# Attention in a two-layer backbone: the third key tile's shaping moved behind group 0's fifth block, query roundings and norms one block later

## The chip, the cores and the metric

The kernel runs on one core of a Trainium2 chip. The metric is the time of one execution in microseconds on the device; what is given is the median of several runs. The profile comes from one further execution, recorded by the hardware profiler.

## What is computed

Two layers of a flow-matching backbone over 512 latent tokens with 256 context tokens, width 1024. Layer 0 mixes tokens by attention, layer 1 by retention; each layer has a gated feed-forward part after it. The change concerns layer 0's attention only:

```python
q_x = rope_2d(rms_norm(q_x.reshape(B, S, N_HEADS, HEAD_DIM), q_gain), tables)
k_x = rope_2d(rms_norm(k_x.reshape(B, S, N_KV_HEADS, HEAD_DIM), k_gain), tables)
k_c = rms_norm(k_c.reshape(B, L, N_KV_HEADS, HEAD_DIM), k_gain)
...
p = jax.nn.softmax(jnp.concatenate([s_ctx, s_loc, sink_col], axis=-1), axis=-1)
return (jnp.einsum('bkgqn,bnkd->bqkgd', p[..., :L], v_c)
        + jnp.einsum('bkgqn,bnkd->bqkgd', p[..., L:L + band], vb))
```

There are 16 query heads of 64 elements and 4 key groups, so that a group g serves heads 4g to 4g+3. Latent queries, in blocks of 128, attend to a band of at most 384 latent keys and all 256 context keys; context queries (two blocks) attend to the context alone. Queries and latent keys are normed and rotated (rope); a learned sink enters each softmax.

## The kernel before

The order of instructions on each engine is decided by a scheduler that reads the program top to bottom and fills engines by its own estimates; only the first part of the kernel and one stretch on TensorE have an order written out by hand. The helper `after` (L91) adds an ordering edge, without a wait of its own, from one instruction to another.

*Pools.* `ap` is the working pool with tags such as "tt" and "pr"; `rp` with tag "res" holds residual rows in 12 buffers. A tile taken from a tag waits for an earlier tile of the same buffer to be done with. "res" buffers also take the attention output before the output projection (`o_raw`), and the reloaded residual (`cres`).

*Keys.* Three normed key tiles are kept in `kn`, each 128 x 512: `kn[0]` has the latent keys of groups 0 and 1, `kn[1]` the context keys, `kn[2]` the latent keys of groups 2 and 3. ScalarE squares each into `ksq` (L529) and scales it by the gain (L530). `rope_key` (L532) rotates a tile on VectorE: a shuffle and three two-input operations (L535 to L538). `key_factor` (L540) sums squares with a matmul (L542), gets the norm's factor in `neg_half_rstd` (L194 to L200: ScalarE's ln, exp and square, VectorE's two steps) and multiplies (L545). `key_parts` (L547) splits a group's 64 rows into a rounded part on ScalarE (L550, L551) and a remainder on VectorE (L553, L554), since matmul operands are taken in two parts. All three tiles are shaped before the loop over groups.

*Query tiles.* `make_q(j)` returns four pieces for heads 2j and 2j+1: `first`, `second` and `third` hold the projection of the latent and of the context stream (24 matmuls each, L147 to L149), and `shape` of each, which scales, squares and rotates on ScalarE, VectorE and GpSimd and then rounds: two casts on ScalarE (L598, L599) and two remainders on VectorE (L600, L601) for each stream. `norms` sums squares by 12-column matmuls (L610) and works out the factors and the sink column (L199, L200, L613, L617).

*Blocks.* `attend(g, s, b)` does one block of 128 queries of group g: four heads' scores (`score`: matmuls S at L703, the masked reduction with running lower bound on VectorE at L704, the exponential on ScalarE at L101, the scaling on GpSimd at L717), the transposes (`turn`: L726, copied out by ScalarE and VectorE in turn at L728), and the value products (`output`: pO at L740). Blocks go in the order `latent + context` (L0 to L3, C0, C1) in groups 0 and 1, then L0, L1, C0, L2, L3, C1 in group 2 and C0, L0, C1, L1, L2, L3 in group 3. Behind blocks 1 and 3 of groups 0 to 2 the loop calls `make_q` for the next group's two tiles. `make_q(0)` and `make_q(1)` stand ahead of the loop.

Of the kernel before, what the change touches and what calls it, by code (L numbers as in the profile page):

```python
# [44 lines left out]
PRB = 9  # L45
TTB = 8
# [3 lines left out]
def dit_kernel(ctx, tc, xT, cT, crow, small, consts, masks, tabs0, tabs1, jtab, adaQ, adaN, adaT, wst, out):  # L50
    nc = tc.nc
# [10 lines left out]
    def T(pool, cols, tag, bufs, dt=F32):  # L62
        return pool.tile([P, cols], dt, tag=tag, bufs=bufs, name=tag)
# [309 lines left out]
    raw = []  # L373
# [148 lines left out]


    kx, kc = {}, {}
    kn = [T(ap, 512, "tt", TTB) for _ in range(3)]
    ksq = [T(ap, 656, "pr", PRB)[:, :512] for _ in range(3)]
    off_grid(ap, 16)
    for a, b, o in zip(kn, ksq, (kvx[0], kvc, kvx[1])):
        nc.scalar.activation(b, o, AF.Square)  # L529
        nc.scalar.activation(a, o, AF.Identity, scale=qk_gain[:, 1:2])  # L530

    def rope_key(t):  # L532

        yy = T(ap, 512, "tt", TTB)
        nc.vector.stream_shuffle(yy, t, swap16)  # L535
        nc.vector.tensor_tensor(t, t, rope0[:, 0:512], op=mult)
        nc.vector.tensor_tensor(yy, yy, rope0[:, 512:1024], op=mult)
        nc.vector.tensor_tensor(t, t, yy, op=add)  # L538

    def key_factor(i):  # L540
        tot = pT()
        nc.tensor.matmul(tot, bd, ksq[i], start=True, stop=True)  # L542
        y = T(ap, 656, "pr", PRB)[:, :512]
        neg_half_rstd(y, ksq[i], tot, HD)
        nc.vector.tensor_tensor(kn[i], kn[i], y, op=mult)  # L545

    def key_parts(e, src, tag="k", bufs=8):  # L547
        k1, k2 = T(akv, 512, tag, bufs, F32R), T(akv, 512, tag, bufs, F32R)
        src = src[64 * e:64 * e + 64, :]
        nc.scalar.copy(k1[0:64, :], src)  # L550
        nc.scalar.copy(k2[64:128, :], src)  # L551
        hi_same = (k1[0:64, :], k2[64:128, :])[e]
        nc.vector.tensor_tensor(k1[64:128, :], src, hi_same, op=sub)  # L553
        nc.vector.tensor_tensor(k2[0:64, :], src, hi_same, op=sub)  # L554
        return k1, k2

    q, stats = {}, {}

    def make_q(j, raw=None):

        if raw is None:
            w = next_w(ap, 0)
            parts_of = lambda k: (w[0][:, k * P:(k + 1) * P], w[1][:, k * P:(k + 1) * P])
        else:

            rows = [[T(ap, 656, "pr", PRB, F32R)[:, :512] for _ in range(2)] for _ in range(2)]
            for i, (hi, lo) in enumerate(rows):
                split(raw[:, i * 512:(i + 1) * 512], hi, lo)  # L570
            parts_of = lambda k: [t[:, k % 4 * P:(k % 4 + 1) * P] for t in rows[k // 4]]
        qs = T(ap, 64, "qs", 4)[:, 0:36].rearrange("p (f n) -> p f n", f=3)
        sqs, o = [], [None, None]

        def part(s, k0, k1):
            if k0 == 0:
                o[s] = pj(NTOK[s])
            for k in range(k0, k1):
                mm3(o[s], parts_of(k), h[s][k], k == 0, k == KT - 1)

        def shape(s):
            n = NTOK[s]
            sq, qn = t_sq(n), t_hn(n)
            nc.scalar.activation(qn, o[s], AF.Identity, scale=qk_gain[:, 0:1])
            nc.scalar.activation(sq, o[s], AF.Square)
            sqs.append(sq)
            if s == 0:
                sw = t_y(s)
                nc.vector.stream_shuffle(sw, qn, swap16)
                nc.gpsimd.tensor_tensor(qn, qn, rope0[:, 0:512], op=mult)  # L590
                nc.vector.tensor_tensor(sw, sw, rope0[:, 512:1024], op=mult)
                nc.vector.tensor_tensor(qn, qn, sw, op=add)
            qa = T(ap, 512, "q", 9, F32R)
            if s == 0:
                qb = T(ap, 512, "q", 9, F32R)
            else:
                qa, qb = qa[:, 0:SC], qa[:, SC:2 * SC]
            nc.scalar.copy(qa[0:64, :], qn[0:64, :])  # L598
            nc.scalar.copy(qb[64:128, :], qn[64:128, :])  # L599
            nc.vector.tensor_tensor(qa[64:128, :], qn[0:64, :], qa[0:64, :], op=sub)  # L600
            nc.vector.tensor_tensor(qb[0:64, :], qn[64:128, :], qb[64:128, :], op=sub)  # L601
            q[2 * j, s] = qa
            q[2 * j + 1, s] = qb

        def norms():
            tot = pj(12)
            for s, sq in enumerate(sqs):
                for b in range(NTOK[s] // P):
                    c = 8 * s + 2 * b
                    nc.tensor.matmul(tot[:, c:c + 2], sq[:, b * P:(b + 1) * P], bd[:, 0:P:64], start=True, stop=True)  # L610
            y, u, z = qs[:, 0], qs[:, 1], qs[:, 2]
            neg_half_rstd(y, z, tot, HD)
            nc.vector.scalar_tensor_tensor(u, tot, HD * EPS, y, add, mult)  # L613
            ue = u.rearrange("p (b e) -> p e b", e=2)
            for e in range(2):
                hd = 2 * j + e
                nc.vector.tensor_scalar(ue[:, e], ue[:, e], nsink[:, hd:hd + 1], -4.0 / HD, op0=mult, op1=mult)  # L617
                stats[hd] = qs

        def first():  # L620
            part(0, 0, 5)

        def second():
            part(0, 5, KT)
            shape(0)
            part(1, 0, 3)

        def third():
            part(1, 3, KT)
            shape(1)  # L630

        return [first, second, third, norms]
# [124 lines left out]
    def attend(g, s, b):  # L757
        blk = Block(g, s, b)
        for i in range(4):
            blk.score(i)  # L760
        for ki in range(len(blk.keys)):
            blk.turn(ki)
        blk.output()
        return blk.copy
# [13 lines left out]

    for piece in make_q(1):
        piece()  # L780
    rope_key(kn[2])
    key_factor(2)
    for e in range(2):
        kx[2 + e] = key_parts(e, kn[2])


    dec = sm_t[:, C_DEC:C_DEC + 8]
    lg = cp.tile([P, 8], F32, name="lg")
# [26 lines left out]
    def context_out(d, w):  # L815
# [9 lines left out]
    parts_o = [p for sb in ((0, 0, 0), (0, 1, 0), (1, 1, 0), (2, 1, 0), (0, 0, 1), (1, 0, 0), (1, 0, 1),  # L825
                            (2, 0, 0), (2, 0, 1)) for p in splits_o(*sb)]
    PARTS_AT = {(2, 4): 2, (2, 5): 3, (3, 0): 3, (3, 1): 2, (3, 2): 2, (3, 3): 2, (3, 4): 2, (3, 5): 2}
    for g in range(NKV):
        final = g == NKV - 1
        for i, (s, b) in enumerate((latent + context, latent + context, mixed, late)[g]):  # L830
            copy = attend(g, s, b)
            if not final and i in (1, 3):
                for piece in make_q(2 * g + 2 + i // 3):
                    piece()
            if (g, i) >= SPLIT_AT:
                first = len(parts_o) == 18
                for _ in range(PARTS_AT[g, i]):
                    parts_o.pop(0)([copy])
                if first:
                    wo0 = wpos[0]  # L840
                    cres = load_stream(1)
            for d in {3: early[:1], 4: early[1:3], 5: early[3:]}.get(i, ()) if final else ():
                wpos[0] = wo0 + d
                wo_w[d] = next_w(ap, 0)
                context_out(d, wo_w[d])
# [12 lines left out]
    for d4 in range(0, KT, 4):  # L858
# [4 lines left out]
        for d in range(d4, d4 + 4):  # L863
            o = pj(SX)
# [1054 lines left out]
```

## Time and profile before

| what | value |
|---|---|
| runs | 1747.34, 1749.5, 1747.12 us; median 1747.34 us |
| profiled execution: span from first to last instruction | 1744.4 us |
| mean granted clock of TensorE | 0.999 |
| instructions | 27605 |
| data moved | 203.54 MB, mean 117 GB/s |
| stretch of the attention blocks | about 97 to 318 us of the span |

The span is the profiled execution's own time from first to last instruction; the runs' time contains what lies around it as well. In rows of the profile, PE is TensorE's matmuls, PEld its weight loads, DVE is VectorE, ACT is ScalarE, POOL is GpSimd, SP is SyncE. "L12" is line 12 of the kernel; a helper's line stands for all who call it, so a tile's name tells them apart. A bracket or an arrow "<-" behind a time names what ended the idle time ahead of the instruction.

### The profile page before, as it was taken

What the parts mean: (1) busy time and instruction counts of PE and PEld (TensorE: products, weight loads), DVE (VectorE), ACT (ScalarE), POOL (GpSimd) and SP (SyncE); (2) the same over time, 40 slices, a digit from 0 to 9 for tenths busy, and PEclk for the clock granted to TensorE, in tenths of its full rate; (3) what the DMA queues carried; (4) which work ended last, traced back from release to release, by engine and by line L of the source; (5) the groups of instructions that cost most, each with busy time, mean ns of one, the idle gap of its engine ahead of it and who ended that gap; (6) DMA issues with size and microseconds to landing.
All of it is one profiled execution on the core that took longest, in us unless ns stands there. A gap on an engine that the chain in (4) does not pass through costs nothing.

```text
span 1744.4 us, 27605 instructions
## 1 busy us (share of the span) xinstructions
PE 1712.7 (98%) x10876; PEld 1527.8 (88%) x10876; DVE 1350.5 (77%) x2368; ACT 846.3 (49%) x1492; POOL 131.0 (8%) x270
## 2 busy tenths in 40 slices
PE   7999999999999999999999999999999999999999
PEld 5777777899999999999988888898898899999997
DVE  6697778788778788787889858758768798777774
ACT  5576667465433334342456534525525565445442
POOL 0035435000000000000000000000000000000000
PEclk9999999999999999999999999999999999999999
DMA  9501012533243534343423524423423224233322
GB/s 353 230 13 38 13 43 68 204 122 135 71 147 121 158 109 145 123 153 101 156 99 86 182 84 130 162 86 121 157 85 118 76 84 132 77 117 101 104 79 85
DMA packets 59602, 203.54 MB, mean 117 GB/s; under 512 B 6608, under 2 KB 6992, under 8 KB 59216
## 3 DMA queue, kind: packets, MB, share of 16 engines
q1 hardware_dynamic: 51984, 175.03, 30.9%
q0 software_dynamic: 7200, 26.22, 5.2%
q8 instruction: 85, 1.39, 0.3%
q10 hardware_dynamic: 288, 0.52, 0.1%
q14 instruction: 45, 0.37, 0.1%
HBM read 199.65 MB, written 2.10 MB: 116 GB/s over the span
## 4 chain that ended last, share of the span: by engine, by line
PE 80%; DVE 8%; DMA 5%; ACT 3%; issue 2%; POOL 1%; SPq 0%; ACTq 0%; POOLq 0%; DVEq 0%
PE Y L886 15%; PE Z L886 7%; PE pj L147 6%; PE pj L148 6%; PE pj L149 6%; PE Z L1268 6%; PE X L886 4%; PE Y L1257 3%; PE pj L1268 2%; PE pT L726 2%; PE X L1257 2%; DMA wraw<-in_wst_dram 2%; PE pO L740 2%; PE S L703 2%; DMA adan<-in_adaQ_dram 1%
## 5 line engine op out<-in xcount | busy, mean ns | idle before, releaser
L164 ACT CAST whi<-wraw 128x1024 fp32r<-128x1024 f32 x258 | 270.2, 1051 | 370.7 <-PE Z L149 88.5
L165 DVE TENSOR_TENSOR wlo<-wraw,whi 128x1024 fp32r<-128x1024 f32 x258 | 315.0, 1223 | 60.9 <-ACT whi L164 59.7
L886 PE MATMUL Y<-aq,whi 128*128 128x384 f32 x640 | 173.7, 335 | 0.5 <-ACT sq L1044 0.5
L256 DVE SCALAR_TENSOR_TENSOR res<-pj,mod,res 128x512 f32<-128x512 f32 (+1 forms) x112 | 81.5, 729 | 65.6 <-PE pj L149 65.0
L886 PEld LDWEIGHTS Y<-aq,whi 128*128 128x128 f32 x640 | 116.6, 188 | 1.7 <-ACT sq L1044 0.9
L273 DVE CUSTOM_DVE_ANT_0 y<-adaw,crow,small_sb 128x1024 bf16<-128x1024 f32 x64 | 81.9, 1280 | 36.0 <-DMA adaw<-in_adaT_dram 35.7
L886 PE MATMUL Y<-aq,wlo 128*128 128x384 f32 x320 | 107.0, 334 | 0.0
L101 ACT ACTIVATE pr<-pr,stat,qs 128x513 f32<-128x513 f32 (+2 forms) x96 | 74.4, 777 | 23.5 <-DVE stat L710 22.9
L1268 PE MATMUL Z<-whi,sA 128*128 128x512 f32 x256 | 81.0, 391 | 1.2 <-ACT gate L1454 1.2
L717 POOL TENSOR_SCALAR pr<-pr,stat 128x512 f32<-128x512 f32 (+2 forms) x96 | 70.2, 744 | 79.5 <-DVE stat L714 54.8
L147 PE MATMUL pj<-ax,whi 128*128 128x512 f32 x176 | 68.8, 391 | 0.1
L149 PE MATMUL pj<-ax,whi 128*128 128x512 f32 x176 | 68.7, 390 | 0.0
L148 PE MATMUL pj<-ax,wlo 128*128 128x512 f32 x176 | 68.5, 389 | 0.0
L147 PE MATMUL pj<-act,whi 128*128 128x512 f32 x168 | 66.0, 393 | 0.0
L148 PE MATMUL pj<-act,wlo 128*128 128x512 f32 x168 | 65.9, 392 | 0.0
L149 PE MATMUL pj<-act,whi 128*128 128x512 f32 x168 | 65.5, 390 | 0.0
L270 POOL DMA_DIRECT2D adaw<-in_adaT_dram x48 | 25.6, 533 | 514.9 <-DVE mod L273 413.6
L726 PE MATMUL pT<-const_sb,pr 128*128 128x128 f32 x352 | 57.4, 285 | 6.1 <-POOL pr L717 3.6
L886 PE MATMUL Y<-sA,whi 128*128 128x256 f32 x304 | 60.6, 282 | 0.2 <-ACT res L1721 0.2
L886 PEld LDWEIGHTS Y<-aq,wlo 128*128 128x128 f32 x320 | 60.1, 188 | 0.0
L726 PEld LDWEIGHTS pT<-const_sb,pr 128*128 128x128 f32 x352 | 39.1, 142 | 23.0 <-POOL pr L717 12.4
L1268 PEld LDWEIGHTS Z<-whi,sA 128*128 128x128 f32 x256 | 48.0, 188 | 11.7 <-ACT gate L1454 1.9
(576 smaller groups left out, 5150.3 us busy)
## 6 DMA issues: line engine op xcount, KB each, us to landing
wraw<-in_wst_dram SPq DMA_DIRECT2D x224, 512.0 KB, 3.7
adaw<-in_adaT_dram POOLq DMA_DIRECT2D x48, 512.0 KB, 3.9
wx<-in_wst_dram SPq DMA_DIRECT2D x30, 512.0 KB, 4.3
adan<-in_adaQ_dram SPq DMA_DIRECT2D x16, 512.0 KB, 8.5
adan<-in_adaN_dram SPq DMA_DIRECT2D x12, 512.0 KB, 7.8
adaw<-in_adaT_dram SPq DMA_DIRECT2D x8, 512.0 KB, 3.9
res<-in_xT_dram SPq DMA_DIRECT2D x14, 256.0 KB, 3.8
aq<-in_adaN_dram SPq DMA_DIRECT2D x12, 256.0 KB, 5.8
```

The lines of the kernel that those rows point to most:

```text
L101: ins = nc.scalar.activation(*args, **kw)
L147: nc.tensor.matmul(o, whi, xhi, start=first, stop=False)
L148: nc.tensor.matmul(o, wlo, xhi, start=False, stop=False)
L149: return nc.tensor.matmul(o, whi, xlo, start=False, stop=last)
L164: after(nc.scalar.copy(hi, t), behind)
L165: return nc.vector.tensor_tensor(lo, t, hi, op=sub)
L256: return nc.vector.scalar_tensor_tensor(res[d], o, mods[l, s][:, part, d:d + 1], res[d], mult, add)
L273: res.append(nc.vector.tensor_tensor_reduce(junk, w, cr[:, s * 1024:(s + 1) * 1024], 1.0, sm_t[:, C_ADAB + l * 48 + j:C_ADAB + l * 48 + j ...
L726: nc.tensor.transpose(tp[:, a * P:(a + 1) * P], self.pr[(0, 2, 1, 3)[a]][:, ki * P:(ki + 1) * P], ident)
L886: nc.tensor.matmul(o, p, r, start=first and k + i == 0, stop=k == 3 and i == 2, skip_group_check=not first)
L1257: ins = nc.tensor.matmul(o[:, e * SC:(e + 1) * SC], p[:, ws], r, start=first and k + e + i == 0, stop=k == 3 and i == 2, skip_group_check= ...
L1268: ins = nc.tensor.matmul(os[t], p, r, start=first and k + i == 0, stop=k == 3 and i == 2, skip_group_check=by_k or not first)
```

## The change

It changes four things in the attention stage. `kn[2]` and `ksq[2]` are taken from "res" in the pool `rp` in place of "tt" and "pr" in `ap`, as are the two scratch tiles of their shaping. The third key tile's rotation, factor and parts stand in the loop behind block 4 (C0) of group 0, its shuffle ordered behind that block's copy. Query tiles made in the loop leave their roundings out of `shape`; the roundings run at the start of `norms`. And that piece runs behind the next block, its first cast of each stream ordered behind that block's copy. Tiles 0 and 1 are made as before. The number of operations on data is the same.

```diff
-    kn = [T(ap, 512, "tt", TTB) for _ in range(3)]
-    ksq = [T(ap, 656, "pr", PRB)[:, :512] for _ in range(3)]
+    kn = [T(ap, 512, "tt", TTB) for _ in range(2)] + [T(rp, 512, "res", 12)]
+    ksq = [T(ap, 656, "pr", PRB)[:, :512] for _ in range(2)] + [T(rp, 512, "res", 12)]
...
-    def rope_key(t):
+    def rope_key(t, room=(ap, 512, "tt", TTB), behind=()):
-        yy = T(ap, 512, "tt", TTB)
-        nc.vector.stream_shuffle(yy, t, swap16)
+        yy = T(*room)
+        after(nc.vector.stream_shuffle(yy, t, swap16), behind)
...
-    def key_factor(i):
+    def key_factor(i, room=(ap, 656, "pr", PRB)):
-        y = T(ap, 656, "pr", PRB)[:, :512]
+        y = T(*room)[:, :512]
...
-    def make_q(j, raw=None):
+    def make_q(j, raw=None, apart=False):
...
+            if apart:
+                rows_of.append(qn)
+            else:
+                two_parts(s, qn)
+
+        def two_parts(s, qn, behind=()):
...
-            nc.scalar.copy(qa[0:64, :], qn[0:64, :])
+            after(nc.scalar.copy(qa[0:64, :], qn[0:64, :]), behind)
...
-        def norms():
+        def norms(behind=()):
+            for s, qn in enumerate(rows_of):
+                two_parts(s, qn, behind)
...
-    rope_key(kn[2])
-    key_factor(2)
-    for e in range(2):
-        kx[2 + e] = key_parts(e, kn[2])
...
+    later = None
     for g in range(NKV):
...
             copy = attend(g, s, b)
+            if later:
+                later([copy])
+                later = None
             if not final and i in (1, 3):
-                for piece in make_q(2 * g + 2 + i // 3):
+                *pieces, later = make_q(2 * g + 2 + i // 3, apart=True)
+                for piece in pieces:
                     piece()
+            if (g, i) == (0, 4):
+                rope_key(kn[2], (rp, 512, "res", 12), [copy])
+                key_factor(2, (rp, 512, "res", 12))
+                for e in range(2):
+                    kx[2 + e] = key_parts(e, kn[2])
```

More of the change, by code (lines that the diff above doesn't have):

```diff
@@ L572, in make_q @@
         qs = T(ap, 64, "qs", 4)[:, 0:36].rearrange("p (f n) -> p f n", f=3)
-        sqs, o = [], [None, None]
+        sqs, o, rows_of = [], [None, None], []
         def part(s, k0, k1):
```

## The prediction

> **What bounds the kernel now.** I read the busy shares and the chain that ended last first, then the attention stage in stretches, then its slices of 10 us, then what TensorE waited for.
>
> ```profile
> span 1744.4 us, 27605 instructions
> PE 1712.7 (98%) x10876; PEld 1527.8 (88%) x10876; DVE 1350.5 (77%) x2368; ACT 846.3 (49%) x1492; POOL 131.0 (8%) x270
> PE 80%; DVE 8%; DMA 5%; ACT 3%; issue 2%; POOL 1%; SPq 0%; ACTq 0%; POOLq 0%; DVEq 0%
> ```
>
> TensorE is 98% busy and holds 80% of the chain. Over the whole span it can gain little; what there is to gain are its gaps. The next rows are stretches of attention: start and end, length, then busy time of PE, PEld, DVE, ACT and POOL, and the granted clock (PEclk) behind them.
>
> ```profile
> core 0: us, PE busy (x) PEld busy (x) DVE busy (x) ACT busy (x) POOL busy (x), PEclk, DMA share, GB/s
> 97.20:148.00 50.80, 46.82 (x318) 36.82 (x316) 41.01 (x111) 34.70 (x73) 22.03 (x44) 1.00 0.07 22
> 148.00:166.00 18.00, 17.91 (x130) 14.78 (x127) 15.47 (x63) 13.45 (x37) 7.61 (x20) 1.00 0.01 1
> 166.00:206.00 40.00, 39.80 (x290) 32.37 (x289) 29.51 (x86) 27.95 (x61) 16.03 (x30) 1.00 0.08 28
> 206.00:254.00 48.00, 46.90 (x324) 37.12 (x324) 35.19 (x118) 30.60 (x74) 22.41 (x46) 1.00 0.12 39
> 254.00:273.00 19.00, 16.59 (x114) 12.45 (x112) 16.79 (x58) 14.71 (x39) 7.02 (x22) 0.91 0.20 56
> 273.00:318.00 45.00, 43.34 (x333) 35.13 (x333) 35.94 (x118) 32.57 (x83) 18.87 (x37) 1.00 0.19 60
> ...
> sum 220.80, PE 211.37 PEld 168.67 DVE 173.90 ACT 153.97 POOL 93.96; mean PE 35.23 PEld 28.11 DVE 28.98 ACT 25.66 POOL 15.66
> ```
>
> In 220.80 us TensorE is idle 9.43 us: 3.98 in the first stretch (group 0), 0.29 in the next two, 1.10, then 2.41 in the short stretch from 254 to 273 (end of group 2), 1.66 at the end. No change that only moves work can take more than these 9.4 us and what the low clock between 254 and 273 costs. The slices show which engine holds TensorE up, and that nothing behind attention gives time back:
>
> ```profile
> 120.00:130.00 10.00, 8.40 (x60) 5.36 (x56) 9.85 (x30) 7.10 (x16) 3.89 (x8) 1.00 0.00 0
> 150.00:160.00 10.00, 9.91 (x73) 8.73 (x73) 9.35 (x42) 8.51 (x26) 3.37 (x10) 1.00 0.00 0
> 160.00:170.00 10.00, 10.00 (x72) 7.16 (x70) 8.80 (x30) 6.46 (x15) 5.72 (x15) 1.00 0.01 2
> 260.00:270.00 10.00, 8.64 (x53) 6.61 (x51) 8.41 (x35) 8.09 (x23) 5.01 (x12) 0.83 0.19 54
> 320.00:330.00 10.00, 10.00 (x46) 8.28 (x45) 6.77 (x10) 6.22 (x7) 0.00 (x0) 1.00 0.90 355
> ```
>
> From 120 to 130 VectorE is 9.85 of 10 busy and TensorE 8.40: in group 0 VectorE is the bound. From 150 to 170 both are nearly full, which is where the change puts the key work. From 320 TensorE is 10.00 of 10, so an earlier end of attention goes through to the end of the kernel. Last, TensorE's waits between 97 and 148 (total, times, longest), and from the timeline the largest later one (start, length, the wait in brackets):
>
> ```profile
> PE pT L726 <- POOL pr L717: 1.7, 3, 0.7
> PE pj L610 <- ACT sq L585: 1.2, 2, 0.7
> PE pT L726 <- ACT tt L728: 0.8, 2, 0.6
> PE pO L740 <- ACT tt L728: 0.2, 1, 0.2
> ...
> 259.65 0.47 PE L703 MATMUL S<-kc,q 128*128 128x256 f32 x2 [1.05 <-DVE qs L200]
> ```
>
> The first four sum to 3.9 us, all the idle time of that stretch.
>
> **The change part by part.** Nothing is added or removed: the same shuffles, products, copies and matmuls run in another order, and two tiles live in another pool.
>
> *Third key tile, away from group 0.* Its work is listed by these rows (for one line: minimum, median and maximum ns, and the first and last start; for a group: busy us, then mean ns):
>
> ```profile
> L535 DVE STREAM_SHUFFLE tt<-tt 128x512 f32<-128x512 f32 x1 | 0.7, 722 | 0.0
> L536 DVE TENSOR_TENSOR tt<-tt,rope x2: 693/693/693, 71.1 to 76.2; 128x512 f32<-128x512 f32 x2
> L200 DVE SCALAR_TENSOR_TENSOR pr<-pr x3: 672/685/693, 78.0 to 104.3; 128x512 f32<-128x512 f32 x3
> L545 DVE TENSOR_TENSOR tt<-tt,pr x3: 685/693/693, 79.2 to 105.0; 128x512 f32<-128x512 f32 x3
> L553 DVE TENSOR_TENSOR k<-tt,k x4: 685/690/1677, 81.8 to 109.3; 64x512 fp32r<-64x512 f32 x4
> L550 ACT CAST k<-tt x4: 604/612/618, 80.2 to 107.2; 64x512 fp32r<-64x512 f32 x4
> ```
>
> On VectorE: one shuffle 0.72, three products of the rotation at 0.69, three steps of the factor (L199, L200, L545) at 0.69, four remainders (L553, L554) at 0.69: 0.72 + 10 x 0.69 = 7.6 us. ScalarE has four casts at 0.61 and three steps of the factor, put at 0.65 as my estimate from the casts and the 0.63 of L529 below: 4.4 us; TensorE has one matmul of the factor. Only the shuffle and rotation, 2.8 us, run early (76 to 79 us); factor and remainders, the other 4.8 us, run at 103 to 110, where VectorE is the bound.
>
> *Query tile 2, one block later.* Per query tile:
>
> ```profile
> L600 DVE TENSOR_TENSOR q<-hn,q 64x512 fp32r<-64x512 f32 x8 | 5.7, 717 | 2.3 <-ACT q L598 2.1
> L601 DVE TENSOR_TENSOR q<-hn,q 64x256 fp32r<-64x256 f32 x8 | 3.4, 421 | 0.2
> L598 ACT CAST q<-hn 64x512 fp32r<-64x512 f32 x8 | 4.9, 618 | 8.3 <-DVE hn L592 8.2
> L598 ACT CAST q<-hn 64x256 fp32r<-64x256 f32 x8 | 3.2, 400 | 0.1
> ```
>
> Remainders on VectorE 2 x 0.72 + 2 x 0.42 = 2.3 us, casts on ScalarE 2 x 0.62 + 2 x 0.40 = 2.0 us. Moving them from behind blocks 1 and 3 to behind the next block takes tile 2's 2.3 us out of the stretch where VectorE holds TensorE. Together VectorE has 4.8 + 2.3 = 7.1 us less to do before group 0's fifth block; in the compiled order two weight splits (L165, 1.2 us each as the row of one at 263.93 below) move up into that room, so 4.7 us net. TensorE can get back only its 3.98 us of waits; I take 3.4, since the first norms' wait (half of the 1.2 on sq) belongs to query tile 1, which is shaped as before. Bounds: 0 (another engine paces as before) and 3.98.
>
> *The two tiles moved to the other pool.* ScalarE's ops on the third key (square and gain) needed buffers that the first two keys' ops held in turn:
>
> ```profile
> 67.87 0.27 ACT L318 COPY sq<-pT 128x128 f32<-128x128 f32 x1 [6.09 <-PE pT L315]
> ...
> 70.14 0.63 ACT L529 ACTIVATE pr<-pj 128x512 f32<-128x512 f32 x1
> 70.61 0.73 ACT L530 ACTIVATE tt<-pj,qk_gain 128x512 f32<-128x512 f32 x1
> 71.18 0.66 ACT L164 CAST pr<-wraw 128x512 fp32r<-128x512 f32 x1
> 71.90 0.50 PE L147 MATMUL pj<-h,pr 128*128 128x512 f32 x1
> ```
>
> In the changed order both stand ahead of L318, in ScalarE's 6.09 us of idleness. The weight cast that releases L147 then starts up to 71.18 - 70.14 = 1.04 us sooner. I take 0.9; bounds 0 (weights or h late instead) and 1.04.
>
> *Where the key work lands.* It is queued behind the copy of group 0's fifth block, at 150 to 170, with query tile 3's remainders (2.3). VectorE there is busy 15.47 of 18 from 148 to 166 and 29.51 of 40 after it; 7.6 + 2.3 us more, against 2.53 + 10.49 us of room, fit if TensorE takes other work meanwhile. It can: the projections of query tile 4, 24 matmuls each for two streams, don't need these keys. Behind the waiting shuffle on VectorE are scores of the block C1 and then of group 1; only group 2 reads the new keys. I charge 0.8 us for the stretch, and 0.5 for group 1, where the projections are then used up sooner. Bounds 0 and 5 (rival 2). The scheduler also puts one weight DMA ahead of four loads of the residual on SP's queue; these are read only near 300, so nothing is charged.
>
> *Query tile 7, end of group 2.* These are VectorE rows between 254 and 264:
>
> ```profile
> 255.93 0.68 DVE L600 TENSOR_TENSOR q<-hn,q 64x512 fp32r<-64x512 f32 x1
> ...
> 258.75 0.74 DVE L704 CUSTOM_DVE_ANT_0 pr<-S,mask,qs 128x512 f32<-128x512 f32 x1
> ...
> 263.93 1.21 DVE L165 TENSOR_TENSOR wlo<-wraw,whi 128x1024 fp32r<-128x1024 f32 x1
> ```
>
> The remainders stand between the scores of block L3 (the fourth latent block), and S waits the 1.05 us quoted. In the changed order the remainders come after the copies of L3, and the weight split of 263.93 ahead of L3. So L3 is scored 2.3 us sooner and that wait goes; next late are group 3's first block, whose heads 14 and 15 need the remainders. I take a gain of 1.0, bounds 1.0 lost to 2.4 (all the idle time there) won.
>
> The clock is the other term there: 0.83 of full speed in the slice 260 to 270, so at most 10 x 0.17 = 1.7 us lost; I take it unchanged, since S, transposes and values stay as thin there as they are. [...]
>
> Sum: -3.4 - 0.9 + 0.8 + 0.5 - 1.0 = -4.0 us. The profiled span, 1744.4, is 2.9 us below the median 1747.34 (runs 1747.12 to 1749.5); I take the same distance for the changed kernel: span 1740.4, time 1743.3.
>
> **The rivals.** 0.2% is 3.5 us, about what a measurement here can tell from no change.
>
> 1. *The lead is handed back in groups 0 and 1.* VectorE does the 7.1 us saved early where it is 9.35 and 8.80 of 10 busy; TensorE spends its projections as filler there and has none later. For: those slices. Against: behind them VectorE has room, 29.51 busy of 40 from 166 on. Price: the 3.4 us of group 0 come back as new waits, leaving -0.9 - 1.0 = -1.9 us, 1745.4.
>
> 2. *Slower: the deferred roundings become what the next scores wait for.* The tiles shaped behind the fourth block (3, 5, 7) are rounded one block before the group that reads them; no projections stand between to cover it. The chain is casts 2.0, then remainders 2.3, 4.3 us at each of three group changes, and in group 0 7.6 us of key work queue with it. It decides if TensorE reaches the next group's third head before VectorE reaches the last remainder. If half of each chain shows (3 x 2.15 = 6.5) beside the key work's excess over the 2.5 us of room to 166 (5.1), against the gains 3.4 and 0.9, it is about +7; with only the roundings half exposed, +2.2. I put it at +5, 1752.3. For: 2.41 us of idle time stand already where group 2 ends. Against: VectorE's total there falls, and scores run one block ahead.
>
> 3. *Nothing to be measured:* what is saved before 148 is only the queue ahead of another wait (the 1.7 us on POOL's pr L717 end a chain through ScalarE and POOL that keeps its length); then the sum is -0.9 or less, 1746.4 to 1747.3.
>
> 4. *The clock.* If the drop goes, another 1.7 us are won, 1741.6; if a second appears in the new thin places, 1.7 are lost, 1745.0. It adds to any case.
>
> **How the numbers follow.** The forecast (1743.3, with its clock variants) 0.43; rival 1 0.20; rival 3 0.10; rival 2 0.27. Faster by over 0.2% takes the forecast: its lower half lies well past the bound, its upper part slips under it, which rival 1's lower part makes up: 0.43. Within 0.2%: rivals 1 and 3, 0.30. Slower: 0.27. Low end: all terms at their good bounds, -3.98 - 1.04 - 2.4 - 1.7 = -9.1, 1738.2. High end: just above rival 2's middle, 1752.5; the half of it above, 0.13, and a few hundredths below the low end are left out. Both signs carry chance, so the forecast's own range is 1740.5 to 1745.
>
> **What would show it.** Right: in the changed profile the waits on POOL pr L717 and ACT tt L728 before 140 are nearly gone, TensorE's idle time to the end of group 0's fourth block is under 1 us; L147's first matmul comes near 71.0; the keys' L553 end at 160 to 170 with TensorE over 9.5 of 10; the wait S L703 near 259 is gone. Rival 1: the same, with new idle time of 2 to 4 us between 150 and 200. Rival 2: waits of S L703 on q at the first blocks of groups 1, 2 and 3, over 2 us each. Wrong altogether: VectorE less busy from 100 to 130, but TensorE with the same gaps.

## The result: 0.15% slower, and the profile after

The changed kernel takes 1749.07 us (median of 21 runs, 1746.24 to 1754.27) against 1747.16 us before (21 runs, 1744.81 to 1749.5). The ratio is 1.0015, 95% interval 1.0009 to 1.0021: slower, clear of the measurement's own spread, by 2.6 us if the ratio is taken times 1747 (the medians lie 1.9 us apart). It stays within the 0.2% that I had called "no change", but the forecast was 4 us the other way. The profiled execution has a span of 1747.3 us.

The page of the changed kernel gives the whole:

```profile
span 1747.3 us, 27610 instructions
PE 1717.0 (98%) x10876; PEld 1530.0 (88%) x10876; DVE 1350.2 (77%) x2368; ACT 847.1 (48%) x1492; POOL 132.0 (8%) x270
...
PE 80%; DVE 9%; DMA 5%; ACT 3%; issue 2%; POOL 1%; SPq 0%; ACTq 0%; DVEq 0%; POOLq 0%
```

The counts of matmuls and of VectorE's and ScalarE's instructions are those of before. PE's busy time is 4.3 us longer for the same 10876 matmuls: part of them ran at a lower clock (0.997 of full speed in the mean of the profile, 0.999 before). The same stretches as in the prediction:

```profile
core 0: us, PE busy (x) PEld busy (x) DVE busy (x) ACT busy (x) POOL busy (x), PEclk, DMA share, GB/s
97.20:148.00 50.80, 49.62 (x349) 40.51 (x349) 36.75 (x113) 33.15 (x72) 18.75 (x42) 1.00 0.07 22
148.00:166.00 18.00, 17.41 (x113) 13.52 (x112) 16.56 (x50) 14.55 (x37) 9.45 (x18) 1.00 0.10 30
166.00:206.00 40.00, 38.72 (x280) 30.65 (x279) 34.30 (x107) 27.96 (x64) 17.54 (x35) 1.00 0.09 27
206.00:254.00 48.00, 46.76 (x322) 36.68 (x322) 36.80 (x119) 32.41 (x74) 21.14 (x47) 1.00 0.04 12
254.00:273.00 19.00, 17.01 (x108) 12.41 (x105) 14.50 (x51) 13.03 (x35) 6.43 (x16) 0.82 0.29 88
273.00:318.00 45.00, 41.01 (x314) 33.60 (x313) 35.37 (x116) 32.62 (x83) 21.04 (x39) 1.00 0.19 63
```

Group 0 is what was forecast: TensorE idle for 1.18 us to 148 where it was 3.98, with VectorE's 41.01 us down to 36.75. Then the gain is spent: 0.59 idle from 148 to 166 (0.09 before), 1.28 to 206 (0.20), about the same to 254, a clock of 0.82 in place of 0.91 to 273, and 3.99 idle in the last stretch where it was 1.66.

To see where a lead comes and goes when projections move between blocks, I follow one number: the start of each block's value products (pO) against before, less the difference in matmul time that TensorE had issued ahead of that point. The matmul time is counted by the spacing of unbroken runs in the trace: 229 ns for 512 columns, 176 for 384, 118 for 256, 80 for 128, 112 for the norms' two. It is counted from ScalarE's copy L318 on, which stands at 67.87 us before and at 68.42 in the changed kernel. Up to that copy TensorE starts the same 710 matmuls in the same order in every kernel of this document, and yet the copy stands anywhere from 66.93 to 69.33 us in the seventeen profiles: what is won or lost ahead of it differs between profiles of kernels that are alike up to there, and is not put down to the change. The lead is worked out from the two traces; minus is ahead.

```
block        g0.L1  g0.L3  g1.L1  g2.L0  g2.L2  g3.C0  g3.L3
before at    127.9  146.4  179.0  222.2  255.3  276.5  316.5
after at     123.4  140.4  184.3  223.8  252.9  277.9  319.0
lead (us)     -4.6   -4.9   -3.1   -2.1   -1.5   -0.1   +1.9
```

The lead of 4.9 us was there at 140 us. It lost 1.8 where the key work lands and group 1 starts, 1.0 in group 1, 0.6 in most of group 2, 1.5 at its end, and 2.0 in group 3, which the prediction had not touched at all. In the waits of TensorE, this is the first stretch (97 to 148) and the last (275 to 325) of the changed kernel:

```profile
PE S L711 <- DVE q L606: 0.9, 1, 0.9
PE pT L734 <- POOL pr L725: 0.2, 1, 0.2
...
PE pT L734 <- POOL pr L725: 3.4, 4, 1.4
PE pO L748 <- DVE stat L718: 0.4, 1, 0.4
```

and the last one of the kernel before:

```profile
PE pT L726 <- POOL pr L717: 1.4, 4, 0.5
```

The waits for POOL's scaling (L717, now L725) are nearly gone from group 0 (0.2 us of 1.7 is left), and in group 3 they are 2.0 us larger than before. How they come about is read on VectorE. Before, a softmax's reciprocal (L714) stands ahead of the split of an output (L165, h<-pO), which must wait for value products; GpSimd's two scalings are in between:

```profile
301.67 0.16 DVE L714 RECIPROCAL stat<-stat 128x2 f32<-128x2 f32 x1
...
301.92 1.76 POOL L717 TENSOR_SCALAR pr<-pr,stat 128x640 f32<-128x640 f32 x2 [1.12 <-DVE stat L714]
...
302.41 0.28 DVE L165 TENSOR_TENSOR h<-pO,h 128x128 fp32r<-128x128 f32 x1
```

In the changed kernel it stands behind it; VectorE, GpSimd and then TensorE, each from its own timeline:

```profile
304.38 0.29 DVE L165 TENSOR_TENSOR h<-pO,h 128x128 fp32r<-128x128 f32 x1 [1.09 <-ACT h L164]
304.59 0.15 DVE L722 RECIPROCAL stat<-stat 128x2 f32<-128x2 f32 x1
...
304.92 2.63 POOL L725 TENSOR_SCALAR pr<-pr,stat 128x640 f32<-128x640 f32 x2 [2.38 <-DVE stat L722]
...
307.60 0.44 PE L734 MATMUL pT<-const_sb,pr 128*128 128x128 f32 x2 [1.01 <-POOL pr L725]
```

VectorE is idle 1.09 us ahead of the split, a reciprocal of 0.15 us stands behind that, GpSimd is idle 2.38 us until it comes, and TensorE waits 1.01. The order is not the whole of it: the same two scalings take 2.63 us here and took 1.76 before, and nothing here shows why. The change edits no line of this stretch, so the other order is the scheduler's.

### The profile page after: what moved, and what is told of

Read it like the earlier page. It is cut to its first block, busy times and chain, and to the rows that moved or that the text cites. A ratio compares the mean times of both kernels' runs of the same rounds, so it can differ in the third digit from the quotient of the medians.

```text
span 1747.3 us, 27610 instructions
## 1 busy us (share of the span) xinstructions
PE 1717.0 (98%) x10876; PEld 1530.0 (88%) x10876; DVE 1350.2 (77%) x2368; ACT 847.1 (48%) x1492; POOL 132.0 (8%) x270
## 4 chain that ended last, share of the span: by engine, by line
PE 80%; DVE 9%; DMA 5%; ACT 3%; issue 2%; POOL 1%; SPq 0%; ACTq 0%; DVEq 0%; POOLq 0%
PE Y L899 14%; PE Z L899 7%; PE pj L147 6%; PE pj L149 6%; PE pj L148 6%; PE Z L1281 6%; PE X L899 3%; PE Y L1270 3%; DMA wraw<-in_wst_dram 2%; PE pj L1281 2%; PE pT L734 2%; PE X L1270 2%; PE pO L748 2%; PE X L147 2%; PE X L149 1%
## 5 line engine op out<-in xcount | busy, mean ns | idle before, releaser
L165 DVE TENSOR_TENSOR wlo<-wraw,whi 128x1024 fp32r<-128x1024 f32 x258 | 314.8, 1223 | 59.5 <-ACT whi L164 58.5
L725 POOL TENSOR_SCALAR pr<-pr,stat 128x512 f32<-128x512 f32 (+2 forms) x96 | 67.6, 717 | 78.4 <-DVE stat L722 66.8
L147 PE MATMUL pj<-ax,whi 128*128 128x512 f32 x176 | 68.7, 391 | 0.0
L147 PE MATMUL pj<-act,whi 128*128 128x512 f32 x168 | 66.0, 393 | 0.0
L899 PE MATMUL Y<-hx,whi 128*128 128x256 f32 x304 | 57.9, 280 | 0.1
```

The costliest lines, as they stand in the source:

```text
L147: nc.tensor.matmul(o, whi, xhi, start=first, stop=False)
L165: return nc.vector.tensor_tensor(lo, t, hi, op=sub)
L899: nc.tensor.matmul(o, p, r, start=first and k + i == 0, stop=k == 3 and i == 2, skip_group_check=not first)
```

## The experiments

Two kinds of number are given: the ratio to the kernel before in runs on the same chip, with its 95% interval, and the lead at some blocks, by the count above, from one profile each. Kernels whose programs are the same up to a block agree in their leads there to about 0.2 us, with one exception: the profile of group 1 deferred with the keys moved has a low clock at 99 to 106 us that no other has (at 103 to 104 us its 512-column matmuls start 0.43 us apart, from 106 us on 0.23), and its leads are not used. At the end of attention ten of the other fifteen leads agree with the ratios to 0.8 us, and all to 2.1. Where the expectations below speak of a lead, it is counted without L318: their 5.9 at group 0's fourth block is 5.3 here, their 3.9 at L2 is 3.4. The ratios come from four chips, so two of them are told apart only where their intervals are.

**The parts, one by one.** The edits are put against the changed kernel.

The keys' move alone:

```diff
-                *pieces, later = make_q(2 * g + 2 + i // 3, apart=True)
-                for piece in pieces:
+                for piece in make_q(2 * g + 2 + i // 3):
```

> Only the third key tile's move (its tiles in the other pool, its shaping behind group 0's fifth block); all query tiles rounded and normed at once, as before the change. Theory A (the deferred roundings are to blame: they stand behind the copy that the next scores need): the lead of group 0 stays but for the roundings' share, 3 us at the fifth block, and little is handed back later: 2 to 4 us faster than before. Theory B (the keys land where VectorE is full): a lead of some 3 us at group 0's fourth block, lost by group 1's first block: 0 to 2 us slower than before. Theory C (the losses behind group 1 come from where the scheduler happens to put weight splits and output splits, and from the clock, not from either part): lead as in A at group 1, and a change of up to 2 us either way in groups 2 and 3 that neither part explains.

Measured: 1.0014 (1.0005 to 1.0022), slower. The lead at g0.L3 is 5.3 us, more than the whole change has. It is 3.7 at g1.L0, 2.2 at g1.L1, and at g1.L2 it is gone, 1.6 behind; from there about 2.5 behind to the end of attention. That is neither A nor C, and B holds late: the loss stands mainly at two waits of 1.3 and 1.8 us, 176 and 194 us, and in a clock of 0.83 from 190 to 200 (at most 1.7). The larger wait, GpSimd and TensorE in their timelines:

```profile
191.05 1.79 POOL L590 TENSOR_TENSOR hn<-hn,rope 128x512 f32<-128x512 f32 x1 [2.06 <-DVE stat L722]
192.82 3.45 POOL L725 TENSOR_SCALAR pr<-pr,stat 128x640 f32<-128x640 f32 x4
...
194.20 0.66 PE L734 MATMUL pT<-const_sb,pr 128*128 128x128 f32 x4 [1.83 <-POOL pr L725]
```

GpSimd's part of a query tile's rotation, 1.79 us, stands ahead of the scalings that TensorE's transposes need, and by then the projections are out: ahead of g1.L1 this kernel has issued 6.3 us more matmul time than before.

The deferral alone, keys and pool as before:

```diff
-    kn = [T(ap, 512, "tt", TTB) for _ in range(2)] + [T(rp, 512, "res", 12)]
-    ksq = [T(ap, 656, "pr", PRB)[:, :512] for _ in range(2)] + [T(rp, 512, "res", 12)]
+    kn = [T(ap, 512, "tt", TTB) for _ in range(3)]
+    ksq = [T(ap, 656, "pr", PRB)[:, :512] for _ in range(3)]
...
+    rope_key(kn[2])
+    key_factor(2)
+    for e in range(2):
+        kx[2 + e] = key_parts(e, kn[2])
...
-            if (g, i) == (0, 4):
-                ...
```

> Only the query tiles' roundings and norms one block later; the third key tile in its old pool and shaped ahead of the loop. Theory A: slower than before by 2 to 5 us, waits of S on the remainders at the first blocks of groups 1, 2 and 3. Theory B: faster by 1 to 2 us, the lead of tile 2's 2.3 us of VectorE kept. Theory C: within 2 us of before, with group 3 in a different order again.

Measured: 1.0032 (1.0019 to 1.0044), by its sign as theory A has it. But the place is not A's: no wait of S on remainders stands at the groups' first blocks, and the first loss is in group 0 itself, where the deferral was to help. A lead of 2.3 at g0.L1 is 0.5 behind at g0.L3. VectorE and TensorE there:

```profile
129.97 1.20 DVE L165 TENSOR_TENSOR wlo<-wraw,whi 128x1024 fp32r<-128x1024 f32 x1
131.09 0.41 DVE L763 COPY res<-pO 128x256 f32<-128x256 f32 x1
131.42 0.15 DVE L722 RECIPROCAL stat<-stat 128x2 f32<-128x2 f32 x1
...
133.62 0.44 PE L734 MATMUL pT<-const_sb,pr 128*128 128x128 f32 x2 [1.08 <-POOL pr L725]
```

A weight split of 1.20 us, for a projection further on, stands ahead of a reciprocal that TensorE needs by way of GpSimd. The place that the remainders left was filled with longer work, less urgent than what came behind it.

The pool alone (shaping ahead of the loop, nothing deferred):

```diff
     for piece in make_q(1):
         piece()
+    rope_key(kn[2])
+    key_factor(2)
+    for e in range(2):
+        kx[2 + e] = key_parts(e, kn[2])
...
-                *pieces, later = make_q(2 * g + 2 + i // 3, apart=True)
-                for piece in pieces:
+                for piece in make_q(2 * g + 2 + i // 3):
...
-            if (g, i) == (0, 4):
-                ...
```

> Only the pool of the third key tile and its square is changed; its shaping stays ahead of the loop and its scratch tiles stay in the old pool; no query tile is deferred. By the prediction's step: L147's first matmul 0.9 us earlier (71.0 in place of 71.9) and the whole 0 to 0.9 us faster. If the lead is lost before group 0's first block: no change in the milestones from 119 us on.

Measured: 0.9988 (0.9979 to 0.9997), 2.1 us faster: the only part of the change that is a gain by itself. ScalarE and TensorE in the changed kernel, to set against the rows of the prediction (with the pool alone L147 stands at 71.38, 3.36 behind L318 at 68.02):

```profile
68.42 0.27 ACT L318 COPY sq<-pT 128x128 f32<-128x128 f32 x1 [2.32 <-PE pT L315]
...
70.69 0.65 ACT L164 CAST pr<-wraw 128x512 fp32r<-128x512 f32 x1
...
71.77 0.80 PE L147 MATMUL pj<-h,pr 128*128 128x512 f32 x1
```

From L318 to the cast it is 2.27 us, before 71.18 - 67.87 = 3.31: the 1.04 us are there, but L147 stands 3.35 behind L318 in place of 4.03, so the step gives 0.7 and not 0.9. The lead is 1.9 to 2.1 us from g0.L1 to g2.L2, more than the step, and 0.2 in the profile at attention's end; the runs have it faster all the same.

The last of the four, pool and deferral with the keys ahead of the loop:

```diff
     for piece in make_q(1):
         piece()
+    rope_key(kn[2])
+    key_factor(2)
+    for e in range(2):
+        kx[2 + e] = key_parts(e, kn[2])
...
-            if (g, i) == (0, 4):
-                ...
```

> Third key tile in the other pool, shaped ahead of the loop, and all query tiles of the loop deferred: the changed kernel without the key move. With the pool alone (0.9988), the pool and the keys (1.0014) and the whole change (1.0015) it completes the four. If what each part costs adds up: about +0.01% over the pool alone, 0.999. If the deferral costs by itself and only the key move's loss in group 1 hides it: 3 to 6 us slower than the pool alone, 1.001 to 1.003.

Measured: 1.0023 (1.0013 to 1.0033). Against the pool alone, the keys' move costs 0.26%, the deferral 0.35%, both together 0.27%. The parts do not add up; each is a cost on top of the pool, and once one of them is paid the other adds nothing that these intervals can tell.

**Where the keys land.** Keys moved, nothing deferred, and

```diff
-            if (g, i) == (0, 4):
+            if (g, i) == (1, 1):
```

with (1, 2) and (1, 4) in two more kernels.

> The third key tile's move alone (no query tile deferred), but behind the second block of group 1 (L1) in place of the fifth of group 0. If the 7.6 us of VectorE work landing at 155 to 168 cost the 6 us that the move alone lost in group 1, the loss at the two waits near 175 and 194 goes away or moves: 2 to 4 us faster than the move alone. If the loss comes of the projections being used up ahead of time as filler in group 0, the waits near 175 and 194 stay and it is as slow as the move alone.

> The same with the key work behind group 1's third block (L2), where VectorE was 4.98 of 10 busy from 190 to 200 in the kernel before. Landing theory: the lead of 5.9 us at group 0's fourth block lasts into group 2, some 4 us faster than before (1741 to 1743). Filler theory: lost in group 1 as before, no faster than 1745.

> The same with the key work behind group 1's fifth block (C0), one block ahead of the group that reads it, 200 to 215, where VectorE was 9.20 and 8.34 of 10 busy. Landing theory: the lead lasts to group 1's end and is lost at group 2's first blocks, within 2 us of before. Filler theory: lost in group 1 already.

Measured: behind (1, 1) 0.9988 (0.9979 to 0.9996), behind (1, 2) 0.9990 (0.9982 to 0.9999), behind (1, 4) 1.0006 (0.9997 to 1.0015), where (0, 4) gave 1.0014. Leads:

```
keys behind   g0.L3  g1.L1  g1.L2  g1.C1  g2.L0  g2.L2  g3.C0  g3.L3
(0, 4)         -5.3   -2.2   +1.6   +2.5   +2.7   +2.5   +2.5   +2.5
(1, 1)         -5.3   -4.7   -1.4   -1.0   -1.6   -1.8   -0.1   -0.1
(1, 2)         -5.3   -4.7   -3.4   -2.8   -3.4   -3.4   -0.9   -0.9
(1, 4)         -5.3   -4.7   -3.8   -1.7   +2.7   +4.1   +1.5   +0.8
```

Most of the lead goes where the key work lands, whichever block that is, or soon behind it: 6.8 us from g0.L3 to g1.L2 for (0, 4), 3.3 from g1.L1 to g1.L2 for (1, 1), 1.3 there for (1, 2), 4.4 from g1.C1 to g2.L0 for (1, 4). The three dear places each show a clock of 0.83 in one slice behind the landing, and (1, 2) does not. First (1, 1) and then (1, 2), from 190 to 200, and (1, 4) from 215 to 225:

```profile
190.00:200.00 10.00, 7.89 (x51) 5.89 (x52) 9.33 (x21) 8.07 (x20) 7.41 (x11) 0.83 0.18 53
```
```profile
190.00:200.00 10.00, 10.00 (x78) 8.06 (x79) 8.61 (x16) 8.13 (x17) 3.99 (x7) 1.00 0.01 2
```
```profile
215.00:225.00 10.00, 7.93 (x53) 7.35 (x50) 9.68 (x17) 5.83 (x13) 1.61 (x1) 0.83 0.01 2
```

For (1, 2) the key work begins at 194.8, and with TensorE 10.00 of 10 busy its first part is hidden; where VectorE was 9.33 or 9.68 busy, TensorE ran thin. So the landing theory holds in the main; for (1, 1) the key work was done by 186 us, and that the low clock 10 us later comes of it is argued, not shown. The filler theory is part of it: only (0, 4) had 7.5 us more matmul time out ahead of g1.L0, the others 1.1, so it was the landing there that drew the projections out. Still (1, 2) is not worth the 4 us expected: 2.5 of its 3.4 go at the end of group 2.

The same place with the deferrals kept:

> The whole change with its deferrals, but the key work behind group 1's third block. If the stretch 150 to 170 was where the change lost its lead, this keeps 1.7 us more than the changed kernel at group 1's first block and ends 1 to 2 us faster than it, 1746 to 1748 where before is 1747. If the deferral's losses in group 2 and 3 stay, it is slower than the same place without deferral (0.9990) by 2 to 4 us.

Measured: 1.0027 (1.0016 to 1.0037), so 0.37% slower than without them. The better place for the keys doesn't save the change.

**Which deferral costs.** The deferral was kept in some groups only:

```diff
-                *pieces, later = make_q(2 * g + 2 + i // 3, apart=True)
+                if g < 2:
+                    *pieces, later = make_q(2 * g + 2 + i // 3, apart=True)
+                else:
+                    pieces = make_q(2 * g + 2 + i // 3)
                 for piece in pieces:
```

with `g < 2` (groups 0 and 1, keys as in the change), `g == 1` (keys as in the change), and on the kernel with the pool alone `g == 0` and `g == 2`.

> The whole change, except that group 2 rounds and norms its two query tiles (6 and 7) at once, as before the change. Theory A: the 2 us lost between group 2's fourth block and group 3's first block come back, 2 us faster than the changed kernel. Theory B: same as the changed kernel, the loss is at group 0's end. Theory C: groups 0 and 1 as in the changed kernel; behind them the order differs again, so a time between 1745 and 1750 that goes with the waits of group 3 and with the granted clock.

> The whole change with the deferral kept for group 1 alone (tiles 4 and 5); groups 0 and 2 round at once. The two waits that cost the move alone 6 us in group 1 stand beside the shaping of tiles 4 and 5. If the deferral helps there, as the whole change's milestones suggest (it lost 1.7 us over the same blocks), this keeps the 5.9 us of lead and is 2 to 5 us faster than before. If a deferral costs wherever it stands, it is slower than the move alone, 1749 to 1751.

> The pool's change, keys ahead of the loop, and the deferral in group 0 alone (tiles 2 and 3). My prediction gave this deferral 2.3 us of VectorE's time in group 0 and so part of the 3.4 us gained. If that holds: 1 us or more ahead of the pool alone at group 0's fourth block. If the room is filled by the weight splits, as the whole deferral's trace shows at 130: no lead over the pool alone, up to 1 us behind it, and the order of group 3 as before.

> The pool's change, keys ahead of the loop, and the deferral in group 2 alone (tiles 6 and 7). All three kernels with the deferral in every group lost 2.0 us between group 3's first and last block and none without it in group 2 lost any. If that loss belongs to group 2's deferral: 2 us lost in group 3 here too, and the whole 2 to 4 us slower than the pool alone (1.000 to 1.001 of before). If it belongs to the deferrals together: group 3 as before, about 0.999.

Measured: groups 0 and 1 with the keys 1.0004 (0.9996 to 1.0013); group 1 with the keys 1.0019 (1.0010 to 1.0028); group 0 on the pool 1.0010 (1.0001 to 1.0018); group 2 on the pool 1.0010 (1.0001 to 1.0020). On the pool, each of the two deferrals is a cost against the kernel without it (0.9988). With the keys at (0, 4) nothing can be told apart: group 1 deferred (1.0019) and groups 0 and 1 deferred (1.0004) lie on either side of none deferred (1.0014), and both intervals overlap with its own.

Two of these answer questions. Group 0's deferral gives no lead at all: 2.0 us at g0.L3, as with the pool alone, and nothing is left of it at g1.L1. And group 2's deferral makes the loss in group 3. With it alone the lead goes from 1.0 behind at g3.C0 to 3.0 behind at g3.L3, and the waits of TensorE from 275 to 325 are the changed kernel's again:

```profile
PE pT L734 <- POOL pr L725: 3.3, 4, 1.4
PE pO L748 <- DVE stat L718: 0.4, 1, 0.4
```

Without it, in the kernel with groups 0 and 1 deferred, they are those of before and the lead stays within 0.2 of before's through all of group 3:

```profile
PE pT L734 <- POOL pr L725: 1.4, 4, 0.5
```

All five kernels with group 2 deferred (the change, the deferral alone, pool and deferral, keys at (1, 2) with deferral, group 2 alone) lost 2.0 us from g3.C0 to g3.L3.

**The thin stretch at the end of group 2, and the clock.** Tile 7's third projection piece and its norms were put one block later, so that matmuls of the projection stand between L2 and group 3, first with the keys at (1, 2) and on the pool alone, neither with a deferral:

```diff
-                for piece in make_q(2 * g + 2 + i // 3):
+                pieces = make_q(2 * g + 2 + i // 3)
+                rest = pieces[2:] if (g, i) == (2, 3) else []
+                for piece in pieces[:len(pieces) - len(rest)]:
                     piece()
+            if (g, i) == (2, 4):
+                for piece in rest:
+                    piece()
```

> The key work behind group 1's third block, no deferral, and query tile 7's third projection piece and norms one block later (behind group 2's fifth block): 10 matmuls of the projection come between the value products of L2 and L3, where there were none. If the low clock at 257 to 263 comes of the stretch without projections, the drop there gets shorter or goes and the lead of 3.9 us at L2 lasts: 1 to 2 us faster than without. If the drop comes whatever fills the stretch: no change, or slower by the later tile 7 (waits of S at group 3's first block).

> The pool's change alone, with tile 7 split in the same way; here the order gives 3 matmuls of the projection between the value products of L2 and L3. By the same reasoning little is changed: within 1 us of the pool alone, 0.998 to 0.9995 of before.

Measured: 0.9971 (0.9960 to 0.9982), 5.1 us faster than before and the best of all, and 0.9974 (0.9964 to 0.9983). The second was a miss: 3 matmuls between two value products looked like little, but 0.14% more, 2.4 us, were won than by the pool alone (0.9988; the two intervals overlap). The slice from 260 to 270 of the first, the second, and the changed kernel:

```profile
260.00:270.00 10.00, 9.30 (x75) 7.04 (x73) 9.16 (x35) 8.47 (x26) 5.39 (x17) 1.00 0.19 53
```
```profile
260.00:270.00 10.00, 9.22 (x71) 6.81 (x69) 9.80 (x41) 8.44 (x27) 4.02 (x14) 1.00 0.13 31
```
```profile
260.00:270.00 10.00, 8.65 (x45) 6.00 (x45) 7.04 (x24) 8.08 (x22) 4.70 (x12) 0.66 0.01 5
```

The clock is 1.00 in both, where before had 0.83 and the changed kernel 0.66; they start 75 and 71 matmuls in the 10 us, the changed kernel 45, partly because a slow clock lets fewer start (0.43 us from one 512-column matmul to the next in the low stretch at 99 to 106 us named above, 0.23 behind it). The split takes the waits and the low clock away together; what each is worth is not told apart. Of the clock it is at most 1.7 us against before, from 3.4 us at half speed.

Last, the same split in the changed kernel, in place of group 2's deferral:

> The whole change, with tile 7 not deferred but split: its third projection piece and its norms behind group 2's fifth block, tile 6 at once. If the thin stretch from L2 to group 3 and its low clock are what turns the change's lead into a loss: the 2.0 us that the kernel without deferral in group 2 lost there do not come, the mean clock is 0.998 or more, and it is 2 us or more faster than before (0.9985 or less). If the lead is gone by group 1's end in any case, within 1 us of before.

Measured: 0.9976 (0.9966 to 0.9985), 4.2 us faster than before, by the lead 3.5 us ahead at g3.L3. The kernel that differs only in the split (groups 0 and 1 deferred) was at 1.0004 and 0.1 behind. So the end of group 2 decides between loss and gain, and the lead is not gone by group 1's end: it was 2.0 at g2.L0 and 4.6 at g2.L3. Without the split, a kernel that comes to g2.L2 ahead loses most of that by g3.C0 whether it defers there or not: 1.5 us in the changed kernel, 2.0 with groups 0 and 1 deferred, 1.7 with the pool alone, 2.5 with the keys at (1, 2).

## Why the prediction was wrong

The sum said -4.0; the lead at attention's end came out at +1.9, and the runs at +2.6. Two steps failed: the end of group 2, wrong in sign, and group 3, which the sum put at nothing.

*Group 0, -3.4 with -0.9 ahead of it:* right in size, -4.9 at g0.L3, of which 0.7 is the step ahead of L147, and the waits named went (3.9 to 1.1 us). TensorE's idle time accounts for 2.8 of the other 4.2; where the rest comes from was not looked into. The reason was half right. I had divided the 7.1 us of VectorE time between keys and tile 2; the deferral in group 0 gives nothing (2.0 with and without it), and the keys' move alone gives 3.3 over the pool's 2.0. Deferral on top of the moved keys takes 0.4 of it away (5.3 to 4.9).

*Where the key work lands, +0.8:* 1.8 from g0.L3 to g1.L1. But the kernel with the same deferrals and the key work at (1, 2) loses 0.7 over these blocks as well (4.9 to 4.2), so that the key work's own share is about 1.1, and the rest goes with the deferral, which on the pool alone, in group 0, loses 2.0 here. The room I had reckoned with, 2.5 us to 166 and 10.5 to 206, was VectorE's idle time. That it was not idle when a score's step was due is my reading, from TensorE's waits, most of them on GpSimd's scalings and on copies (1.7 us from 148 to 206, none before); the queue was not followed there row by row. *Group 1, +0.5:* 1.0.

*End of group 2, -1.0:* wrong in sign, +1.5. The wait of S that I quoted did go (its row names L200, a step of the norms that stood behind the remainders), as did the remainders ahead of the scores, but other waits took its place (2.8 us of waits between 206 and 275, 3.0 before), and the low clock, which I had taken as unchanged, lasts twice as long. The slice's 0.66 is 6.8 us at half speed, where 0.83 is 3.4. Nor is the loss the deferral's alone: without it in group 2, 2.0 us go there. The step looked at the edit and not at the thin stretch, where a lead won earlier is lost. The low clock is rival 4's bad side, and it is hardly one profile's chance. Mean granted clock over 21 runs of the changed kernel is 0.9970; over 27, 33, 20 and 26 runs of before beside the experiments it is 0.9982 or 0.9983. A share of 0.0012 of 1747 us is 2.1 us of lost clock, 4.2 us more at half speed. That is an upper bound of the price, since TensorE also waits in that time; among the changed kernel's own runs 0.001 of clock goes with 1.2 us. So 1.4 to 2.1 of the 2.6 us may go with the clock. Where in the kernel the mean was lost is not on record but for the profiles: 3.4 us at half speed between 19 and 26 us of the span, outside attention, also stand in ten of the seventeen, the changed kernel's among them (0.76 over those 7 us) and before's not (1.00). The kernels with tile 7 split have 0.9988, 0.9992 and 0.9990.

*Group 3, not in the sum:* +2.0. I costed the edits where they stand and compared the orders there; a scheduler that fills queues by its own estimates can give another order to everything behind, and group 2's deferral alone does it (2.0 us there in all five kernels that have it).

Of the rivals, 2 had the right culprits, the deferrals and the key work, but the wrong mechanism: no chain of casts and remainders shows at the heads of groups 1, 2 and 3. Rival 1 (handed back in groups 0 and 1) holds for 2.8 of the 4.9 us. The chance of 0.30 on "within 0.2%" is where the result lies, near its upper end.

On the clock, the traces show when it fell, and no run shows what sets it off. The longest wait of TensorE between 206 and 275 is 1.05 us in the kernel before and 0.8 us in the changed one, and in both the granted clock fell to 0.50, for 3.4 us and for 6.8. What stands ahead of the fall is thin: 3.41 us up to it, as long as the low stretch of before, and then the low stretch, first before, then changed:

```profile
258.06:261.47 3.41, 2.02 (x11) 1.22 (x9) 3.38 (x17) 2.54 (x7) 0.17 (x1) 1.00 0.00 0
261.47:264.88 3.41, 3.23 (x14) 2.99 (x15) 2.86 (x12) 2.75 (x9) 2.53 (x4) 0.50 0.02 5
```
```profile
257.80:261.21 3.41, 2.12 (x11) 1.18 (x9) 3.03 (x17) 2.74 (x9) 1.31 (x3) 1.00 0.63 224
261.21:268.04 6.83, 6.13 (x26) 4.37 (x28) 4.27 (x12) 5.57 (x15) 3.75 (x10) 0.50 0.00 0
```

The profiles have sixteen such falls in attention. In the 3.4 us ahead of fourteen of them TensorE was busy for 1.34 to 2.19 us with 7 to 15 matmuls, ahead of the other two for 2.56 and 2.79 with 22 and 24; in the changed kernel, each of the two stretches of that length before it holds 30. It is no rule yet: a stretch as thin, 1.92 us and 15 matmuls at 129.4 to 132.8 of the deferral alone, had no fall behind it (the clock is 1.00 from 97 to 148 there). How thin is too thin stays open.

What stays open too is why the parts don't add up. That the order of what follows differs is shown by the traces; which order results was not predicted by anything tried here.

## What to carry to other kernels

Taking work from a busy engine pays only if what moves into its place is more urgent than what left; look at which short instruction stands behind each long one in an engine's order (here a reciprocal of 0.15 us behind a split of 1.20), not only at the engine's idle share. When a scheduler makes the order, compare the order of everything behind an edit, to the end of the stage, before summing up the edit. A stretch with few matmuls cost twice here, by its waits (2.8 us between 206 and 275 in the changed kernel) and by the clock of 0.50 that followed (6.8 us); keeping a little filler work for it was worth 2.4 to 4.9 us, more than any of the moves ahead of it.

## What the runs showed of the hardware

TensorE's granted clock fell to 0.50 behind stretches that were thin but not idle (2.02 us of matmuls in 3.41 in the kernel before, 2.12 in the changed one): for 3.4 us in the kernel before and 6.8 in the changed one. In the kernel with group 2 alone deferred 0.09 and 0.42 are missing in two slices, 1.8 and 8.4 us if all of it is at half speed, 10.2 in sum:

```profile
250.00:260.00 10.00, 9.36 (x68) 7.41 (x66) 7.92 (x29) 6.40 (x17) 2.10 (x7) 0.91 0.42 133
260.00:270.00 10.00, 9.04 (x45) 6.25 (x45) 6.49 (x19) 7.16 (x19) 4.78 (x14) 0.58 0.00 0
```

PE reads 9.04 of 10 busy in the second with 45 matmuls, where the first has 9.36 with 68: slow matmuls count as busy, so the busy share hides the loss, and the granted clock beside it tells.
